# Hybrid attention block on one core: five edits to the order of loads and of VectorE's work (second gate's weights, a third memory weight buffer, the third operand, the end, a half tile)

## The chip, the cores and the metric

The kernel runs on one core of a Trainium2 chip. The metric is device time in microseconds (us). "The time before" is the median of three runs of the kernel before; beside it stands one profiled execution, from which every duration in this document comes.

The core has five engines, each with an instruction stream of its own that is worked off in order: TensorE (PE, matrix multiplies), VectorE (DVE), ScalarE (ACT), GpSimd (POOL) and SyncE (SP), which here only issues transfers. A transfer may also be issued by ScalarE. Engines wait for one another by semaphores.

## The reference, cut to what matters

The input `x` has 1024 rows of width 1024. After an rms norm it is multiplied by one wide weight matrix, and the columns of the product feed three mixers, their gates, and the gates of the merge:

```python
h = rms_norm(x, g_pre[layer])
a_qkv, bq, bk, bv, mq, ga, gb, gm, mg = jnp.split(h @ w_in[layer], split_at, axis=-1)
# A: three groups of heads, dilated windows, merged by a softmax over the groups' log denominators
for gi, (window, dil) in enumerate(A_GROUPS):
    o_g, lse_g = dilated_window_attention(aq[:, :, hs], ak[:, :, hs], av[:, :, hs], window, dil)
wts = jax.nn.softmax(jnp.stack(lses, axis=0), axis=0).astype(dt)
oa = jnp.einsum('gbsh,gbshd->bshd', wts, jnp.stack(outs, axis=0)).reshape(b, s, BRANCH_WIDTH)
# B: grouped queries, rms norms on q and k, axial rope
ob = lax.map(attend, q_blocks).transpose(1, 0, 2, 3, 4, 5).reshape(b, s, B_Q)
# M: cross attention into 256 memory rows
kvm = rms_norm(mem, g_mem[layer]) @ w_mem_kv[layer]
om = jnp.einsum('bhsn,bnhd->bshd', pm, vm).reshape(b, s, M_Q)

ya = (oa * jax.nn.silu(ga)) @ w_br_a[layer]
yb = (ob * jax.nn.silu(gb)) @ w_br_b[layer]
ym = (om * jax.nn.silu(gm)) @ w_br_m[layer]
gates = jax.nn.sigmoid((mg + b_merge[layer]).astype(jnp.float32)).astype(dt).reshape(b, s, N_BRANCHES, d)
merged = gates[:, :, 0] * ya + gates[:, :, 1] * yb + gates[:, :, 2] * ym
x = x + rms_norm(merged @ w_out[layer], g_post[layer])
```

Everything is float32.

## The kernel before, in words

**Arithmetic.** A float32 operand is split into a high part, rounded to the type that TensorE multiplies, and a low part, the rest: ScalarE copies the high part out (`wh`, `hh`), VectorE subtracts it (`wl`, `hl`; both in `split`, L105 to L107). A product is three matmuls: high x high, high x low, low x high. So each weight tile that arrives from memory costs one ScalarE and one VectorE instruction before TensorE can use it. `wr` is the tag of raw weights on arrival, with `WR = 2` buffers; `wh` and `wl` have two each.

**Order.** All of ScalarE's, VectorE's, POOL's and TensorE's work in the parts that the change touches is issued in the order in which the program text issues it (`manual_schedule`). SP's queue is in text order too: a transfer whose buffer isn't free yet holds what stands behind it.

**The start.** `xT` comes in eight tiles `xk[k]` of 128 x 1024 (L448 to L455), tile 0 in two halves; the first half of tile 0 and the whole of tile 1 are issued by ScalarE, all else by SP, between pieces of the weights `wb` of the key and value projection. `x_tile(k)` (L278) splits a tile into `hh[k]`, `hl[k]`, in halves of 512 columns. TensorE runs `kv_proj` (L364): for each `k`, eight row blocks of three 128 x 256 matmuls. Meanwhile the same rows come again in row layout, and ScalarE sums their squares (`row_squares`); POOL makes `rcol` from them (`rstd_cols`), a mean, a power of -0.5, and further small steps. VectorE makes the tables `Ck` and `Sk`, and POOL `Cq` and `Sq`, from one load `bt` (L465).

**The first weave.** L493 runs two gate units on TensorE, two halves of 24 matmuls of 128 x 512 each (`dense`, L140 to L148). Each half ends in a PSUM bank of tag `d`, of which there are two; VectorE empties it into a tile `gth` (L223). A unit's weights are loaded from `wu` and split by `prepare(n)` (L156), which `run_items` calls for unit n and unit n + 1 when unit n begins. Between the matmuls goes other work (`kv_gen`, L407): the key norms `k_norm` (L333: a Square on ScalarE, a sum on VectorE, four small steps `kss` on POOL, products with the tables on VectorE) and the preparation of the memory, `mem_prep` (L383), which reads the transposed memory tiles `mt` (L491) and loads the memory rows into `mr` to sum their squares (L269, L270). After the weave VectorE multiplies the keys by POOL's `kss` (`kn_mult`, L400).

**The memory units.** The second weave (L562) runs eight units `add_kv(u)` of 24 matmuls of 128 x 256 (L537) and one unit of queries. `kv_prep(u)` (L507) loads the unit's weights `wmem[u]` into a `wr` buffer and splits them (L512, L513). In units 1 to 4 a leftover of a gate unit is finished too (`gates_left`): ScalarE's tanh, a product on VectorE, and a store of `gth` to `g2d` (L229), on SP.

**The last item of mixer A.** Mixer A works on 12 items, each in four steps (loop L1751 to L1779): exponentials, scores, masks of the next blocks, transposes `tr` of the probabilities (L1530), copied out as `app` by VectorE (L1534) or ScalarE (L1536), and the values (`pv`, L1539), which fill a `d` bank that ScalarE copies out to `og` (L1560). Behind each step stands filler work, `fill(n)`: n matmuls of the branch products (L1315), which use the same two `d` banks and are emptied by VectorE (L1321). `other(n, j)` (L1661) hangs small work on step j of item n: among it the gated operand k of the branch product, a load (`a_load`), a multiply (`a_mult`, L1597) in place in the tile `ot`, and a split into `hh[k]`, `hl[k]` (`a_split`). Behind the last step (q == NQS) come the turning of the log denominators, `last_weights` (small VectorE steps ending in `leg`), `fill(8)`, and the spreading of the weights by TensorE (`spread`, L1742).

**The end.** The last output block (n = 3, u = 1) is summed and squared in pieces (`piece`, L2060). Its rms norm is a mean of three partial sums (`mean`, L1927 and L1929, on tiles of 128 x 1 in `hbm`), a power on POOL (`root`, L1933), and a product with the residual added (`send_part`, L1962), stored in parts by SP and ScalarE. The gain is multiplied in ahead of that, in three column ranges (`gain`, L1958).

Of the kernel before, what the change touches and what calls it, by code (L numbers as in the profile page):

```python
# [8 lines left out]
F32 = mybir.dt.float32  # L9
# [6 lines left out]
S = 1024  # L16
NT = 8
P = 128
# [32 lines left out]
def block(ctx: ExitStack, tc: tile.TileContext, x, xT, memT, mem, cst, msk, bcst, tabA, gpost,  # L51
          wu, wv, wb, wmem, wbr, wout, out):
    nc = tc.nc
# [4 lines left out]
    wp = ctx.enter_context(tc.tile_pool(name="wp", bufs=2))  # L58
# [20 lines left out]
    def pss1():  # L79
        return bank["p"].tile([P, 512], F32, name="s1", tag="s1", bufs=bank["n"][1])  # L80
# [75 lines left out]
    def prepare(n):  # L156
        if n == len(queue) and n in early and n not in ready:
            ready[n] = early[n]()
        if n < len(queue) and n not in ready:
            ready[n] = queue[n][0]()  # L160
# [84 lines left out]
    def pool(name, side="left"):  # L245
        p = tc.tile_pool(name=name, bufs=1, side=side, reuse_waits="tile")
        return p, p.__enter__()
# [6 lines left out]
    startp, st = pool("start")  # L254
# [10 lines left out]
    xk = [st.tile([P, S], F32, name=f"xk{k}") for k in range(8)]  # L265
# [98 lines left out]
    def kv_proj():  # L364
        banks = [pss1(), pss1(), pss1(), pso()]
        th, tl = wkv
        for k in range(8):
            for T in range(NT):
                dst = banks[T // 2][:, T % 2 * 256:T % 2 * 256 + 256]
                t = slice(T * 128, T * 128 + 128)  # L370
                for i, (a, b) in enumerate([(hh[k][:, t], th[:, k]), (hl[k][:, t], th[:, k]), (hh[k][:, t], tl[:, k])]):
                    PE.matmul(dst, a, b, start=k == 0 and T % 2 == 0 and i == 0, stop=k == 7 and T % 2 == 1 and i == 2)
        return banks
# [74 lines left out]
    for k in range(8):  # L448
        if k in WKV:
            load_wkv(k, WKV[k])  # L450
        if k == 4:
            nc.sync.dma_start(cs, cst)
        for e in range(2 if k == 0 else 1):
            t = slice(e * 512, e * 512 + 512) if k == 0 else slice(0, S)
            (nc.scalar if (k, e) in ((0, 0), (1, 0)) else nc.sync).dma_start(xk[k][:, t], xT[k, :, t])  # L455
    bt = st.tile([P, 1024], F32, name="bt")
    ET = mybir.EngineType
    manual = tc.manual_schedule(engines={ET.Activation, ET.DVE, ET.Pool})
# [26 lines left out]
    table("Ck", B_COS, B_KN, V)  # L485
    table("Sk", B_SIN, B_KS, V)
    banks = kv_proj()
    mt = []
    for c in range(2):
        t = st.tile([P, 4, 256], F32, name=f"mt{c}", tag=f"xk{c}")  # L490
# [14 lines left out]
        V.tensor_copy(mm[1], rows_of(mm[0], 2))  # L505

    def kv_prep(u):  # L507
        raw = wp.tile([P, 1024], F32, name="wr", bufs=WR)
        nc.sync.dma_start(raw, wmem[u])
        wh = wp.tile([P, 1024], R, name="wh")  # L510
        wl = wp.tile([P, 1024], R, name="wl")
        A.activation(wh, raw, AF.Copy)  # L512
        V.tensor_tensor(wl, raw, wh.bitcast(F32), op=OP.subtract)  # L513
        return wh.rearrange("p (k f) -> p k f", k=8), wl.rearrange("p (k f) -> p k f", k=8)
# [291 lines left out]
    lo, hi = half  # L806
# [181 lines left out]
    for n, (i, e, k) in enumerate(steps_v):  # L988
        if k == 0:
            now = v_banks()  # L990
        for j in range(4):
            if i is None:
                t = slice(e * 512 + j * 128, e * 512 + j * 128 + 128)
# [339 lines left out]
    def fill(n):  # L1333
        for _ in range(n):
            next(filler)
        filled[0] += n
# [70 lines left out]
    for f in range(4):  # L1407
        t = t23.tile([P, 2, S], F32, name=f"acc{f}", tag=f"ac{f}")
# [3 lines left out]
    with tc.tile_pool(name="aa", bufs=1, reuse_waits="tile") as aa:  # L1412
# [176 lines left out]
        def a_load(k, both=True):  # L1589
            GG[0, k] = [aa.tile([P, S], F32, name="ot", bufs=2) for _ in range(1 + both)]  # L1590
            for t, src in zip(GG[0, k], (g2d, od)):
                nc.sync.dma_start(t, src[0, k])

        def a_mult(k, o=None, i=slice(0, 64)):
            g_ = GG[0, k][0].rearrange("p (i b) -> p i b", b=16)[:, i]
            o = (GG[0, k][1] if o is None else o).rearrange("p (b i) -> p i b", b=16)[:, i]
            V.scalar_tensor_tensor(g_, o, 0.5, g_, op0=OP.mult, op1=OP.mult)  # L1597

        def a_split(k, t=slice(0, S)):
            assert y_done[0] >= 8  # L1600
            split(hh[k][:, t], hl[k][:, t], GG[0, k][0][:, t])
# [57 lines left out]
        COM = {}  # L1659

        def other(n, j):  # L1661
            p_, g = divmod(n, 3)
            if j == 2:
                if n + 2 < len(items):
                    qk_load(n + 2)
                if n + 1 < len(items):
                    items[n + 1]["values"]()
            if g == 0 and n:
                if j == 0:
                    COM[p_] = combine(p_ - 1)  # L1670
                    COM[p_]["fetch"]()
                elif j == 2:
                    COM[p_]["weights2"]()
                    COM[p_]["load"](0, 1)
            if g == 1 and p_ and j:
                c = COM[p_]
                c["weigh"](j - 1)
                if j == 1:
                    c["load"](2)
                else:  # L1680
                    c["add"](j - 1)
            if g == 2 and j == 0 and 0 < p_ < 3:
                COM[p_]["store"]()
            for k, x in enumerate((0, 1, 2, 4)):
                if (n, j) == (x, 3):
                    b_load(k)
                elif (n, j) == (x + 1, 1):
                    b_split(k)
            for k, q in ((0, 33), (1, 37)):
                x = 4 * n + j - q  # L1690
                if x == 0:
                    a_load(k)
                elif x == 2:
                    a_mult(k)
                elif x == 3:
                    a_split(k)
            if (n, j) == (9, 3):
                a_load(2, False)
            elif (n, j) == (11, 1):
                a_mult(2, COM[3]["ogs"][2])  # L1700
            elif (n, j) == (11, 2):
                a_split(2)
                a_load(3, False)
            if (n, j) == (11, 1):
                lse_load()

# [15 lines left out]
        def last_weights():  # L1722
            mn = cb.tile([P, 2, NT], F32, name="lmn")
            e = cb.tile([P, 3, 2, NT], F32, name="leg")
            dn = cb.tile([P, 3, 2, NT], F32, name="ldn")
            ds_ = cb.tile([P, 2, NT], F32, name="lds")
            V.tensor_tensor(mn, comb[:, 0, :, 0], comb[:, 1, :, 0], op=OP.min)
            V.tensor_tensor(mn, mn, comb[:, 2, :, 0], op=OP.min)
            V.tensor_tensor(e, comb[:, :, :, 0], mn[:, None].to_broadcast([P, 3, 2, NT]), op=OP.subtract)
            A.activation(e, e, AF.Exp, scale=-1.0)  # L1730
            V.tensor_tensor(dn, e, comb[:, :, :, 1], op=OP.mult)
            V.tensor_tensor(ds_, dn[:, 0], dn[:, 1], op=OP.add)
            V.tensor_tensor(ds_, ds_, dn[:, 2], op=OP.add)
            V.reciprocal(ds_, ds_)
            V.tensor_tensor(e, e, ds_[:, None].to_broadcast([P, 3, 2, NT]), op=OP.mult)
            return e
# [14 lines left out]
        for q in range(NQS + 2):  # L1751
            it, j = at(q)
            pr, pj = at(q - 1)
            nx, nj = at(q + 1)
            if it:
                for e in range(2):
                    it["exps"](2 * j + e)
            if nx:
                nx["scores"](nj)
                for e in range(2):  # L1760
                    nx["masked"](2 * nj + e)
            if q == NQS:
                fill(4)
            if pr and q:
                for e in range(2):
                    pr["trans"](2 * pj + e)
            if j == 0 and 0 < q < NQS:
                items[q // 4 - 1]["stats"]()
            if q % 2 and q > 2:
                items[(q - 2) // 4]["pv"]((q - 2) % 4 // 2)  # L1770
            if j == 2 and q // 4 % 3 == 0 and 4 <= q < NQS:
                COM[q // 12]["weights"]()
            if it:
                fill(7 if q % 2 == 0 else 5)
                other(q // 4, j)
            elif q == NQS:
                lse_turn()
                e = last_weights()
                fill(8)  # L1779
        fill(4)  # L1780
        c = combine(3)
# [150 lines left out]
    def root(n, u):  # L1932
        G.tensor_tensor(SS[n, u][:, 3:4], SS[n, u][:, 3:4], mhalf[:, 0:1], op=OP.pow)  # L1933
# [22 lines left out]
    def gain(n, u, c):  # L1956
        r = RES[n, u]
        V.tensor_tensor(r[:, c], r[:, c], gp[:, c], op=OP.mult)  # L1958
# [105 lines left out]
    send_part(3, 0, lo, nc.sync)  # L2064
    piece(0)
    send_part(3, 0, hi, nc.sync)
    gain(3, 1, hi)
    piece(1)
    mean(3, 1, (1, 0))
    gain(3, 1, quarter[0])  # L2070
    mean(3, 1, (2,), False)
    root(3, 1)
    gain(3, 1, quarter[1])
    for c, e in ((hi, nc.sync), (quarter[0], nc.scalar), (quarter[1], nc.sync)):
        send_part(3, 1, c, e)
# [12 lines left out]
WR, KV_STEP, RB_WAIT, KN_PAD = 2, 700, 1500, 2800.0  # L2088
# [119 lines left out]
```

## Time and profile before

| | |
|---|---|
| three runs | 1399.67, 1403.54, 1404.08 us |
| median | 1403.54 us |
| the profiled execution | 1402.44 us, of which its span is 1400.3 us |
| granted TensorE clock, mean | 0.998 |
| transfers | 221.05 MB, 158 GB/s in the mean |

The span runs from the first to the last instruction of the program; the 2.1 us between it and the execution's own time lie around it. Times within the span count from its start. A row of a timeline gives start, duration (both us), engine, line, operation, output <- inputs and shape; the bracket at its end gives how long the engine had stood idle before it and what it had waited for. Small gaps have no bracket, so waits of TensorE are read from the distance between the starts of neighbouring matmuls. A row of the list of waits gives who waited, for whom, and total, count and longest in us. SPq is SP's issuing of a transfer.

### The profile page before, as it was taken

The numbers are of one execution on the slowest core, as the hardware profiler recorded it, in microseconds if no ns is written. First come the engines' busy times: TensorE is split into PE (matmuls) and PEld (weight loads), VectorE is DVE, ScalarE is ACT, GpSimd is POOL, SyncE is SP. The second block draws the span as 40 slices with busy tenths as digits, with TensorE's granted clock in tenths as the row PEclk, the third lists the DMA queues.
The fourth block names the chain that finished last, engine by engine and source line by source line (L and its number), as shares of the span: only waits on it lengthen the run. The fifth ranks groups of instructions, "written<-read, shape, count | busy, mean of one in ns | idle before, by whom it ended". The sixth has DMA issues, their size and how long they took to land.

```text
span 1400.3 us, 21252 instructions
## 1 busy us (share of the span) xinstructions
PE 1383.2 (99%) x7485; PEld 1106.5 (79%) x7485; DVE 977.3 (70%) x1767; ACT 674.6 (48%) x1457; POOL 547.6 (39%) x431
## 2 busy tenths in 40 slices
PE   9999999999999999999999999999999999999997
PEld 8899986666657888888888888888887778778886
DVE  4865458677652387998678777755766656777977
ACT  6644355656653364543222322344446766743453
POOL 1225504676672422267554565423300011245410
PEclk9999999999999999999999999999999999999999
DMA  9432011011005783565555566665567577746613
GB/s 376 141 106 77 16 65 61 17 34 42 17 26 173 265 272 108 177 236 200 140 165 162 166 180 179 204 226 191 200 213 256 175 227 188 256 124 230 228 61 136
DMA packets 108667, 221.05 MB, mean 158 GB/s; under 512 B 20272, under 2 KB 50192, under 8 KB 108560
## 3 DMA queue, kind: packets, MB, share of 16 engines
q1 hardware_dynamic: 94496, 205.14, 45.6%
q10 hardware_dynamic: 14064, 14.55, 3.0%
q8 instruction: 59, 0.97, 0.3%
q14 instruction: 48, 0.39, 0.1%
HBM read 146.97 MB, written 60.09 MB: 148 GB/s over the span
## 4 chain that ended last, share of the span: by engine, by line
PE 85%; DMA 6%; DVE 4%; ACT 2%; issue 2%; SPq 1%; POOL 1%; ACTq 0%; POOLq 0%; DVEq 0%
PE s L1112 35%; PE d L1315 9%; PE s L1901 4%; PE ov L738 4%; PE s L999 3%; PE d L144 3%; PE d L146 3%; PE d L148 3%; PE s L1487 3%; PE d L1550 2%; PE tr L704 2%; PE s L722 2%; PE s L723 2%; PE tr L1530 1%; DMA wr<-in_xT 1%
## 5 line engine op out<-in xcount | busy, mean ns | idle before, releaser
L1112 PE MATMUL s<-T,ch 128*128 128x512 f32 x912 | 215.0, 389 | 0.0
L1112 PEld LDWEIGHTS s<-T,ch 128*128 128x128 f32 x912 | 171.2, 188 | 35.5
L729 POOL TENSOR_TENSOR bl<-bl,bp 128x512 f32<-128x512 f32 x96 | 123.8, 1290 | 48.4 <-ACT bp L725 42.4
L107 DVE TENSOR_TENSOR ch<-sf,ch 128x512 fp32r<-128x512 f32 x102 | 92.6, 914 | 63.2 <-ACT ch L106 63.2
L1112 PE MATMUL s<-hh,ch 128*128 128x512 f32 x408 | 129.8, 389 | 0.0
L1315 PE MATMUL d<-hh,wh 128*128 128x512 f32 x384 | 126.0, 398 | 0.0
L705 DVE TENSOR_REDUCE bn<-tr 128x1 f32<-128x512 f32 x128 | 85.5, 687 | 19.5 <-PE tr L704 18.1
L725 ACT ACTIVATE bp<-s 128x512 f32<-128x512 f32 x128 | 76.0, 597 | 44.9 <-PE s L723 43.2
L1145 POOL TENSOR_TENSOR o<-o,rc 128x1024 f32<-128x1024 f32 x24 | 62.3, 2596 | 70.2 <-DMA o<-rs 53.8
L1112 PEld LDWEIGHTS s<-hh,ch 128*128 128x128 f32 x408 | 76.6, 188 | 15.9
L1177 ACT ACTIVATE sp<-s 128x512 f32<-128x512 f32 x52 | 31.0, 596 | 113.5 <-PE s L1112 93.5
L1315 PEld LDWEIGHTS d<-hh,wh 128*128 128x128 f32 x384 | 72.1, 188 | 15.4 <-issue 0.8
L1322 POOL TENSOR_TENSOR acc<-acc,wl 128x512 f32<-128x512 f32 x32 | 57.1, 1789 | 64.5 <-DVE wl L1321 58.8
L107 DVE TENSOR_TENSOR wl<-wr,wh 128x1024 fp32r<-128x1024 f32 x38 | 51.9, 1365 | 42.6 <-ACT wh L106 40.2
L1112 PE MATMUL s<-hh,wh 128*128 128x512 f32 x208 | 80.9, 389 | 0.0
L1112 PE MATMUL s<-hl,wh 128*128 128x512 f32 x208 | 80.9, 389 | 0.0
L1112 PE MATMUL s<-hh,wl 128*128 128x512 f32 x208 | 80.9, 389 | 0.0
L1112 PE MATMUL s<-hl,ch 128*128 128x512 f32 x204 | 79.4, 389 | 0.0
L106 ACT ACTIVATE wh<-wr 128x1024 fp32r<-128x1024 f32 (+1 forms) x64 | 56.2, 878 | 47.2 <-PE d L1315 15.8
L1505 ACT ACTIVATE pra<-pra,sts 128x192 f32<-128x192 f32 (+2 forms) x176 | 77.4, 442 | 1.6 <-DVE sts L1497 1.6
L1315 PE MATMUL d<-hl,wh 128*128 128x512 f32 x192 | 77.9, 406 | 0.0
L144 PE MATMUL d<-hh,wh 128*128 128x512 f32 x192 | 76.7, 399 | 0.9 <-DVE gth L223 0.9
(415 smaller groups left out, 3599.1 us busy)
## 6 DMA issues: line engine op xcount, KB each, us to landing
wr<-in_wu SPq DMA_DIRECT2D x38, 512.0 KB, 7.2
rw<-in_wu SPq DMA_DIRECT2D x26, 512.0 KB, 5.4
o<-rs SPq DMA_DIRECT2D x96, 128.0 KB, 2.3
qkd<-o SPq DMA_DIRECT2D x24, 512.0 KB, 6.1
wl<-thd SPq DMA_DIRECT2D x24, 512.0 KB, 5.3
thd<-rs ACTq DMA_DIRECT2D x36, 256.0 KB, 2.4
aq<-qkd SPq DMA_DIRECT2D x12, 512.0 KB, 4.6
ak<-qkd SPq DMA_DIRECT2D x12, 512.0 KB, 6.9
```

What stands on the lines that cost most here:

```text
L106: A.activation(dst_h, src, AF.Copy)
L107: V.tensor_tensor(dst_l, src, dst_h.bitcast(F32), op=OP.subtract)
L144: PE.matmul(dst, wh[:, k, :], hh[k][:, t], start=k == 0, stop=False)
L705: fp["last"] = V.tensor_reduce(st[i]["n"][:, j, c:c + 1], s, axis=AX.X, op=OP.min)
L725: A.activation(pp, s, AF.Exp, scale=-1.0)
L729: G.tensor_tensor(lsum[i % 2], lsum[i % 2], pp, op=OP.add)
L738: PE.matmul(o[e * 64:e * 64 + 64], VS[:, kt, kv], d.pop(kt), start=kt < 2, stop=kt >= NT - 2)
L1112: PE.matmul(dst, a, b, start=opens and i == 0, stop=closes and i == 11, skip_group_check=True)
L1145: G.tensor_tensor(QO[n, u], QO[n, u], RT.pop((n, u))[0], op=OP.add)
L1315: PE.matmul(s, a, b, start=q == 0, stop=q == 11)
L1322: G.tensor_tensor(accs[f][:, h], accs[f][:, h], th[:, h], op=OP.add)
L1505: A.activation(src, src, AF.Exp, scale=-1.0, bias=sums(T, h, 0), accum_out=sums(T, h, 1))
```

## The change

It has five edits; line numbers grow by one behind the second.

1. Tile 1 of `xT` is loaded in two halves as tile 0 is: the first by ScalarE, the second by SP.
2. `prepare(1)` stands ahead of the loads of the memory tiles: the second gate unit's weights are loaded and split earlier in the order of SP, ScalarE and VectorE.
3. The third and the sixth memory unit's raw weights go into the buffer `mr`, in which the memory rows were, and no longer into one of the two `wr` buffers.
4. The third operand's multiply is done in two halves, in steps 2 and 3 of the last item and no longer whole in step 1; its split stands behind the last weights and no longer in step 2.
5. At the end, the gain of the last block's second half of columns stands behind the root.

```diff
@@ -450,9 +450,9 @@
             load_wkv(k, WKV[k])
         if k == 4:
             nc.sync.dma_start(cs, cst)
-        for e in range(2 if k == 0 else 1):
-            t = slice(e * 512, e * 512 + 512) if k == 0 else slice(0, S)
-            (nc.scalar if (k, e) in ((0, 0), (1, 0)) else nc.sync).dma_start(xk[k][:, t], xT[k, :, t])
+        for e in range(2 if k < 2 else 1):
+            t = slice(e * 512, e * 512 + 512) if k < 2 else slice(0, S)
+            (nc.scalar if k < 2 and e == 0 else nc.sync).dma_start(xk[k][:, t], xT[k, :, t])
@@ -485,6 +485,7 @@
     table("Sk", B_SIN, B_KS, V)
     banks = kv_proj()
+    prepare(1)
     mt = []
@@ -505,7 +506,7 @@
     def kv_prep(u):
-        raw = wp.tile([P, 1024], F32, name="wr", bufs=WR)
+        raw = st.tile([P, 1024], F32, name="mr", bufs=1) if u % 3 == 2 else wp.tile([P, 1024], F32, name="wr", bufs=WR)
         nc.sync.dma_start(raw, wmem[u])
@@ -1696,11 +1697,10 @@
             if (n, j) == (9, 3):
                 a_load(2, False)
-            elif (n, j) == (11, 1):
-                a_mult(2, COM[3]["ogs"][2])
-            elif (n, j) == (11, 2):
-                a_split(2)
-                a_load(3, False)
+            elif (n, j) in ((11, 2), (11, 3)):
+                a_mult(2, COM[3]["ogs"][2], slice(32 * j - 64, 32 * j - 32))
+                if j == 2:
+                    a_load(3, False)
@@ -1776,6 +1776,7 @@
                 lse_turn()
                 e = last_weights()
+                a_split(2)
                 fill(8)
@@ -2064,12 +2065,12 @@
     piece(0)
     send_part(3, 0, hi, nc.sync)
-    gain(3, 1, hi)
     piece(1)
     mean(3, 1, (1, 0))
     gain(3, 1, quarter[0])
     mean(3, 1, (2,), False)
     root(3, 1)
+    gain(3, 1, hi)
     gain(3, 1, quarter[1])
```

SP's queue from the load of the table `bt` on, of the kernel before (`wu` gate weights, `memT` and `mem` the memory, `wmem` its weights, `g2d` stores of finished gates):

```order
L483 DMA bt<-in_bcst 128x1024
L491 DMA mt_458<-in_memT 128x1024
L491 DMA mt_460<-in_memT 128x1024
L115 DMA wr<-in_wu 128x1024
L269 DMA mr<-in_mem 128x1024
L509 DMA wr<-in_wmem 128x1024 x2
L269 DMA mr<-in_mem 128x1024
L509 DMA wr<-in_wmem 128x1024
L229 DMA g2d<-gth 128x512 x3
L509 DMA wr<-in_wmem 128x1024
L229 DMA g2d<-gth 128x512
```

And with the change:

```order
L483 DMA bt<-in_bcst 128x1024
L115 DMA wr<-in_wu 128x1024
L492 DMA mt_465<-in_memT 128x1024
L492 DMA mt_467<-in_memT 128x1024
L269 DMA mr<-in_mem 128x1024
L510 DMA wr<-in_wmem 128x1024 x2
L269 DMA mr<-in_mem 128x1024
L510 DMA mr<-in_wmem 128x1024
L510 DMA wr<-in_wmem 128x1024
L229 DMA g2d<-gth 128x512 x3
L510 DMA wr<-in_wmem 128x1024
L229 DMA g2d<-gth 128x512
```

The gate weights have moved ahead of the two memory tiles. The third `wmem` load writes to `mr`, behind the second load of memory rows into the same buffer; a fourth `wmem` load now stands ahead of the stores.

TensorE behind the last values of mixer A, with what each row waits for in brackets (`app` transposed probabilities, `avs` values, `hh`/`hl` operands of the branch products, `leg` the last weights), of the kernel before:

```order
L1550 MATMUL d<-app,avs_9520 64x128 [waits DVE_49]
L1550 MATMUL d<-app,avs_9520 64x128
L1315 MATMUL d<-hh_91,wh 128x512 [waits DVE_49]
L1315 MATMUL d<-hl_99,wh 128x512
L1315 MATMUL d<-hh_91,wh 128x512
L1315 MATMUL d<-hh_92,wh 128x512
L1742 MATMUL s_12062<-cs,leg 64x128 x8
```

And with the change:

```order
L1551 MATMUL d<-app,avs_9521 64x128 [waits DVE_49]
L1551 MATMUL d<-app,avs_9521 64x128
L1316 MATMUL d<-hh_91,wh 128x512 [waits Activation_49]
L1316 MATMUL d<-hl_99,wh 128x512
L1316 MATMUL d<-hh_91,wh 128x512
L1316 MATMUL d<-hh_92,wh 128x512
L1742 MATMUL s_12064<-cs,leg 64x128 [waits DVE_49]
L1742 MATMUL s_12064<-cs,leg 64x128 x7
```

The matmuls stand in the same order; the first filler matmul behind the values waits for ScalarE in place of VectorE, and the first spreading matmul has a wait for VectorE of its own.

VectorE at the end, from the first part of the last block but one that is sent (`res` output rows, `on_12606` the gain and `on_12607`/`on_12608` rows of `x`, `wl` the kept sum), of the kernel before:

```order
L1962 SCALAR_TENSOR_TENSOR res<-res,hbm,on_12607 128x512
L1958 TENSOR_TENSOR res<-res,on_12606 128x512
L2061 TENSOR_TENSOR res<-s_13203,wl 128x256
L1927 TENSOR_SCALAR hbm<-hbm 128x1
L1929 SCALAR_TENSOR_TENSOR hbm<-hbm 128x1
L1958 TENSOR_TENSOR res<-res,on_12606 128x256
L1929 SCALAR_TENSOR_TENSOR hbm<-hbm 128x1
L1958 TENSOR_TENSOR res<-res,on_12606 128x256
L1962 SCALAR_TENSOR_TENSOR res<-res,hbm,on_12608 128x512
L1962 SCALAR_TENSOR_TENSOR res<-res,hbm,on_12608 128x256 x2
```

And with the change:

```order
L1963 SCALAR_TENSOR_TENSOR res<-res,hbm,on_12609 128x512
L2062 TENSOR_TENSOR res<-s_13205,wl 128x256
L1928 TENSOR_SCALAR hbm<-hbm 128x1
L1930 SCALAR_TENSOR_TENSOR hbm<-hbm 128x1
L1959 TENSOR_TENSOR res<-res,on_12608 128x256
L1930 SCALAR_TENSOR_TENSOR hbm<-hbm 128x1
L1959 TENSOR_TENSOR res<-res,on_12608 128x512
L1959 TENSOR_TENSOR res<-res,on_12608 128x256
L1963 SCALAR_TENSOR_TENSOR res<-res,hbm,on_12610 128x512
L1963 SCALAR_TENSOR_TENSOR res<-res,hbm,on_12610 128x256 x2
```

The gain of 512 columns has gone from ahead of the last sum to behind the last step of the mean, after which POOL's root starts.

## The prediction

> **What bounds the kernel now.** I read the page's busy times first, then the list of what TensorE waited for, then the places named there. In the first rows the span stands against TensorE's busy time:
>
> ```profile
> span 1400.3 us, 21252 instructions
> PE 1383.2 (99%) x7485; PEld 1106.5 (79%) x7485; DVE 977.3 (70%) x1767; ACT 674.6 (48%) x1457; POOL 547.6 (39%) x431
> ```
>
> TensorE is idle for 17.1 us out of 1400.3, and no edit removes or adds a matmul. So the change can only fill waits of TensorE or shorten the end behind its last matmul. The list of TensorE's waits (total, times, longest, in us) has four rows at places that the change touches:
>
> ```profile
> PE tr L1530 <- DVE app L1534: 1.0, 2, 0.8
> PE d L144 <- DVE gth L223: 0.9, 1, 0.9
> ...
> PE d L537 <- DVE wl L513: 0.8, 1, 0.8
> PE d L537 <- ACT wh L512: 0.7, 1, 0.7
> ```
>
> They add up to 3.4 us. Everything else that I say is about which of them go, and what takes their place.
>
> **Edit 1, the half tile on ScalarE's queue: 0.** The second half of x tile 1 (256 KB) moves from ScalarE's queue to SP's. The stretch view gives 10 to 20 us (columns: length, busy time and instructions of each engine, granted clock, DMA share, GB/s), the timeline two rows of TensorE:
>
> ```profile
> 10.00:20.00 10.00, 10.00 (x90) 10.00 (x90) 9.40 (x15) 8.56 (x15) 0.00 (x0) 1.00 1.04 415
> ```
>
> ```profile
> 6.86 0.39 PE L372 MATMUL s<-wbh,hl 128*128 128x256 f32 x1 [0.41 <-DVE hl L283]
> ...
> 33.62 0.64 PE L275 MATMUL tr<-cs,rcol 128*128 128x128 f32 x4
> ```
>
> The transfer engines are full, so the same bytes take as long in either queue. If the first tile is ready sooner, TensorE starts before 6.86, but it then waits at 33.62 for the row norms, which stand at the end of the same stream (the POOL rows below end them at 33.57). A gain here is therefore lost there. A loss is not: 90 matmuls in 10 us are 0.11 us each, so from 6.86 on the second half of tile 1 is wanted after 36 of them, at 10.8, and from there lateness counts in full. I take 0; bounds -0.2 and +0.6, which is 256 KB at 415 GB/s. [...]
>
> **Edit 2, second gate's weights ahead of the memory tiles: -0.8.** The chain of waits (start, us), then the timelines:
>
> ```profile
> 24.56 10.78 DMA wr<-in_wu
> ...
> 35.36 1.07 ACT wh L106
> ```
>
> ```profile
> 30.76 0.69 DVE L465 TENSOR_TENSOR Ck<-bt,cs 128x512 f32<-128x512 f32 x1 [5.09 <-DMA bt<-in_bcst]
> ```
>
> ```profile
> 31.60 1.97 POOL L131 TENSOR_TENSOR rcol<-rcol,mhalf 128x8 f32<-128x8 f32 x1
> ...
> 35.51 1.10 POOL L465 TENSOR_TENSOR Sq<-bt,cs 128x512 f32<-128x512 f32 x1
> 38.16 0.20 POOL L339 TENSOR_TENSOR kss<-kss,rsq 128x4 f32<-128x4 f32 x1 [1.55 <-DVE kss L338]
> ```
>
> ```profile
> 40.30 0.39 PE L148 MATMUL d<-hh,wl 128*128 128x512 f32 x1
> 41.61 0.50 PE L144 MATMUL d<-hh,wh 128*128 128x512 f32 x1 [0.92 <-DVE gth L223]
> ```
>
> The weights land at 35.34 (24.56 + 10.78), and ScalarE and VectorE stand until then, with the key norms and the first gate's evacuation (gth) queued behind them. TensorE needs that evacuation's bank at 40.53 (40.30 and 0.23 for the matmul) and gets it at 41.61: 1.08 us lost, and 0.1 more in refilling. In the change the weights follow the table bt, which had landed at 30.7; 512 KB at 415 GB/s are 1.26 us, so they land at about 32.0, 3.3 us earlier. VectorE does not gain all of that: its evacuation stands behind a product that waits for POOL's chain from 38.16, and POOL is held by its two tables until 36.6. So at most 38.16 - 36.6 = 1.56 us are free, which would remove the whole stall (-1.2). But VectorE's split, 1.23 us, now runs from 33.1 to 34.3, just as POOL comes from 33.57 to the small steps ahead of the tables. What that does stands elsewhere in the trace:
>
> ```profile
> 120.78 0.27 POOL L318 TENSOR_SCALAR ssb<-ssb,rsq 128x4 f32<-128x4 f32 x1
> ...
> 122.25 1.43 POOL L320 TENSOR_SCALAR ssb<-ssb,rcol 128x4 f32<-128x4 f32 x1
> ```
>
> ```profile
> 121.28 2.35 DVE L107 TENSOR_TENSOR wbl<-wr,wbh 128x1024 fp32r<-128x1024 f32 x2
> ```
>
> Under two such splits a small step of POOL takes 1.43 us in place of 0.27 and ends with the second split (123.63 and 123.68). So POOL loses up to 34.3 - 33.6 = 0.7 us, and its chain starts 0.9 us earlier in place of 1.56. The evacuation then gives the bank free at 41.6 - 0.9 = 40.7, where TensorE wants it at 40.5: -1.0. VectorE's own sums of two SBUF operands, ahead of the evacuation, can be held by the tables in the same way, so I take -0.8; bounds 0 and -1.2. [...]
>
> The memory tiles land one transfer later, some 1.3 us. They are first read by ScalarE behind the key norms, which start earlier too; that covers them.
>
> **Edit 3, a third memory weight buffer: -2.0.** Chain of waits, then TensorE, SP and ScalarE:
>
> ```profile
> 53.88 1.24 DVE wl L513
> 55.14 6.58 DMA wr<-in_wmem
> 61.82 1.07 ACT wh L512
> 62.91 1.24 DVE wl L513
> ```
>
> ```profile
> 61.97 0.28 PE L537 MATMUL d<-mh,wl 128*128 128x256 f32 x1
> 62.93 0.39 PE L537 MATMUL d<-mh,wh 128*128 128x256 f32 x1 [0.69 <-ACT wh L512]
> 63.16 0.28 PE L537 MATMUL d<-ml,wh 128*128 128x256 f32 x1
> 64.19 0.39 PE L537 MATMUL d<-mh,wl 128*128 128x256 f32 x1 [0.76 <-DVE wl L513]
> ```
>
> ```profile
> 50.87 0.33 SPq L509 DMA_DIRECT2D wr<-in_wmem  x1
> ```
>
> ```profile
> 45.48 1.06 ACT L270 ACTIVATE mr<-mr 128x1024 f32<-128x1024 f32 x1 [0.28 <-DMA mr<-in_mem]
> ```
>
> The fourth unit's weights may only be loaded when the second unit's split ends (55.12), take 6.6 us and meet TensorE late. From 61.97 to 64.19, 2.22 us, it issues three matmuls of 0.11: 1.9 us lost, and 0.1 in refilling. In the change the third unit's weights go into the buffer of the memory rows, free from 46.5 (45.48 + 1.06), and the fourth takes the place that the third has in SP's queue now, at 50.87, 4.3 us before 55.14. It then lands by 57.5, and the wait goes. What is late next is the fifth unit, now issued at 55.14 or before: even with 6.6 us it lands by 61.7 and its two splits (1.07, 1.24) end by 64.1. It is wanted 24 x 0.11 = 2.7 us after the fourth starts at 62.1, less the 0.8 of edit 2: at 64.0. So it just fits with the same delay. I take -2.0; bounds -2.0 and 0. SP issues in order, and its wait for ScalarE's square at 46.5 now stands ahead of the fourth unit's load; that load is not due before 50.87, which covers it.
>
> **Edit 4, the third operand in halves and its split later: -0.3.**
>
> ```profile
> 1239.80 2.01 DVE L1597 SCALAR_TENSOR_TENSOR ot<-og,ot 128x1024 f32<-128x1024 f32 x1
> ```
>
> ```profile
> 1241.84 0.38 PE L1530 MATMUL tr<-cs,pra 128*128 128x128 f32 x2
> 1243.04 0.44 PE L1530 MATMUL tr<-cs,pra 128*128 128x128 f32 x2 [0.82 <-DVE app L1534]
> ...
> 1249.55 1.09 PE L1550 MATMUL d<-app,avs 128*64 128x128 f32 x16
> 1250.60 0.50 PE L1315 MATMUL d<-hh,wh 128*128 128x512 f32 x1
> ```
>
> ```profile
> 1250.69 0.60 ACT L1560 ACTIVATE og<-d 128x512 f32<-128x512 f32 x1 [1.94 <-PE d L1550]
> ```
>
> The multiply of 2.01 us stands ahead of the masks and the copy that TensorE waits for at 1243.04. Two transposes take 0.2, the start-to-start is 1.20: 1.0 us lost. In halves, behind those copies, it no longer stands there: -1.0. But the order of the change shows a new wait: TensorE's first filler matmul behind the last values (1250.60) now waits for ScalarE and no longer for VectorE. The only ScalarE step left there is the copy og of the bank just written. It starts 0.05 after the last values end (1250.64) and takes 0.60, so TensorE, ready at 1250.60, could go at 1251.3: +0.7. Sum -0.3; bounds -1.0 (the copy is not what it waits for) and +0.2 (it waits for the evacuation behind the moved split: 1.06 and 1.22 us on ScalarE and VectorE).
>
> **Edit 5, the end's order: -0.3.**
>
> ```profile
> 1393.23 0.68 DVE L1958 TENSOR_TENSOR res<-res,on 128x512 f32<-128x512 f32 x1
> ...
> 1395.82 1.54 DVE L1962 SCALAR_TENSOR_TENSOR res<-res,hbm,on 128x512 f32<-128x512 f32 x3 [0.44 <-POOL hbm L1933]
> ```
>
> ```profile
> 1389.55 0.93 POOL L1933 TENSOR_TENSOR hbm<-hbm,mhalf 128x1 f32<-128x1 f32 x1 [8.75 <-DVE hbm L1929]
> 1395.12 0.67 POOL L1933 TENSOR_TENSOR hbm<-hbm,mhalf 128x1 f32<-128x1 f32 x1 [4.63 <-DVE hbm L1929]
> ```
>
> The gain of 0.68 (0.60 between starts) leaves the place ahead of the last sum and comes behind the mean, so the root starts 0.6 earlier. There it runs beside a wide gain and not a narrow one: 0.93 in place of 0.67. Left: -0.34; bounds -0.6 and 0.
>
> **The sum.** 0 - 0.8 - 2.0 - 0.3 - 0.3 = -3.4 us, since TensorE is full from the places of edits 2 and 3 to the end, and later waits hang on it, not on the clock. The profiled execution took 1402.44 us (span 1400.3), which gives 1399.0. The median shown, 1403.54, would give 1400.1; its runs lie from 1399.67 to 1404.08. I take the middle, 1399.6.
>
> **Rivals.**
> - *The middle gains in full* (0.18): the matmul at 1250.60 does not wait, edit 4 is -1.0 and edit 2 -1.2. For it: VectorE's own release was in time. Against: the wait in the order. 1402.44 - 4.5 = 1397.9, or 1398.5 by the same middle.
> - *The gate stall stays* (0.20): POOL holds the evacuation, edit 2 is 0. For it: even with the gain as reckoned the bank is 0.2 us late. Against: 3.3 us of earlier landing. -2.6: 1400.4.
> - *The third buffer does nothing* (0.07): the fourth unit's weights are still slow, edit 3 is 0. For it: 6.58 us for one load. Against: 4 us of earlier issue. -1.4: 1401.6.
> - *Slower* (0.05): the half tile behind SP's queue misses the first projection. TensorE has no slack from 6.86 to 33.62, so each us after 10.8 costs one. It decides from 3.4 us late, at 14.2; 5 us late, 1404.0, or 1404.6 by the same middle. For it: SP's queue is in order and full. Against: only three small pieces stand ahead of it.
>
> **How the numbers follow.** My forecast has 0.50. A change within 0.3% (4.2 us) is what a measurement here can hardly tell from none. The forecast lies inside that, 0.8 us from its edge, with runs that scatter by 2 us: a third of it falls beyond. Faster by over 0.3%: 0.50 x 0.35 + 0.18 x 0.7 + 0.20 x 0.2 + 0.07 x 0.1 = 0.35. Slower by over 0.3%: 0.03. Within: 0.62. The range is 1396.3 to 1402.9: below, the full middle and the low runs; above, the third buffer's failure.
>
> **What would show it.** Right: the second gate's split on ScalarE near 32, not 35.4; no wait of TensorE at the fourth memory unit; the wait at the transposes of the last item gone and one of some 0.7 us at the filler matmul behind the last values, ended by og; the last root some 0.6 us nearer to the last matmul. Wrong: the wait for gth still near 1 us, or later waits of TensorE that grow by what the first 70 us gained.

## The result, and the profile after

| | kernel before | changed kernel |
|---|---|---|
| median (lowest to highest) of 22 runs each | 1401.17 us (1398.14 to 1405.00) | 1398.53 us (1397.06 to 1402.11) |
| ratio, 95% interval | | 0.9983, 0.9976 to 0.9991 |
| profiled execution, its span | 1402.44, 1400.3 | 1401.02, 1399.2 |

The change makes the kernel faster by 0.17%, some 2.4 us (1.3 to 3.4). The stated range, 1396.3 to 1402.9, holds the time; the sum of the terms was -3.4. By the bound of 0.3% this is no difference, the likeliest of the three outcomes.

The list of TensorE's waits after the change, below its first two rows (who, for whom, total, times, longest in us):

```profile
PE s L1000 <- ACT wh L106: 0.9, 1, 0.9
PE d L1316 <- ACT wh L106: 0.8, 1, 0.8
PE d L1316 <- ACT og L1561: 0.7, 1, 0.7
PE s L1000 <- DVE wh L107: 0.6, 1, 0.6
PE s L1113 <- DVE rs L1158: 0.6, 1, 0.6
```

The four rows on which the prediction rested (tr for app, d for gth, and two for the memory weights wl and wh) are gone. The wait for og, which the order foretold, has come. Three others are new and stand at places that no edit touches: the first row (near 487 us), the second (near 1050) and the last (near 916).

Rows picked from the timeline of the changed kernel, at the gate and at the fourth memory unit:

```profile
32.53 1.06 ACT L106 ACTIVATE wh<-wr 128x1024 fp32r<-128x1024 f32 x1 [1.32 <-DMA wr<-in_wu]
34.17 0.73 POOL L377 TENSOR_TENSOR rsq<-rcol 128x8 f32<-128x8 f32 x1
35.94 0.96 DVE L347 TENSOR_TENSOR kt<-kt,kt 128x256 f32<-128x256 f32 x1
40.45 0.69 DVE L223 TENSOR_TENSOR gth<-d,rb 128x512 f32<-128x512 f32 x1
41.95 0.39 PE L148 MATMUL d<-hh,wl 128*128 128x512 f32 x1
42.18 0.39 PE L144 MATMUL d<-hh,wh 128*128 128x512 f32 x1
50.44 0.33 SPq L510 DMA_DIRECT2D wr<-in_wmem  x1
59.37 1.06 ACT L513 ACTIVATE wh<-wr 128x1024 fp32r<-128x1024 f32 x1 [0.27 <-PE d L538]
62.34 0.28 PE L538 MATMUL d<-mh,wh 128*128 128x256 f32 x1
62.57 0.28 PE L538 MATMUL d<-mh,wl 128*128 128x256 f32 x1
```

The second gate's split runs at 32.53 (35.36 before). The 42.18 row is the matmul that waited until 41.61 before; it follows its forerunner by 0.23, without a wait. The fourth memory unit's split waits for TensorE (for the buffer of split weights) and no longer for a transfer.

At the last item and at the end:

```profile
1241.50 0.60 PE L1531 MATMUL tr<-cs,pra 128*128 128x128 f32 x4
...
1249.30 0.60 ACT L1561 ACTIVATE og<-d 128x512 f32<-128x512 f32 x1 [0.33 <-PE d L1551]
1249.95 0.50 PE L1316 MATMUL d<-hh,wh 128*128 128x512 f32 x1 [0.70 <-ACT og L1561]
...
1393.85 0.93 POOL L1934 TENSOR_TENSOR hbm<-hbm,mhalf 128x1 f32<-128x1 f32 x1 [4.03 <-DVE hbm L1930]
1394.81 1.54 DVE L1963 SCALAR_TENSOR_TENSOR res<-res,hbm,on 128x512 f32<-128x512 f32 x3
```

Two transposes and the two behind them run through (the second pair stood at 1243.04 before); the filler matmul behind the last values waits 0.70 for og, and starts at 1249.95. The last root starts 1.35 behind TensorE's last end (1392.50) in place of 1.95. (Between the two places of edit 4, L1707 to L1777, the change does not shift the line numbers.)

### The profile page after: what moved, and what is told of

It reads as the page before. It is cut to its first block, busy times and chain, and to the rows that moved or that the text cites. A ratio compares the mean times of both kernels' runs of the same rounds, so it can differ in the third digit from the quotient of the medians.

```text
span 1399.2 us, 21259 instructions
## 1 busy us (share of the span) xinstructions
PE 1383.4 (99%) x7485; PEld 1108.6 (79%) x7485; DVE 983.8 (70%) x1768; ACT 673.5 (48%) x1457; POOL 545.1 (39%) x431
## 4 chain that ended last, share of the span: by engine, by line
PE 86%; DMA 5%; DVE 4%; ACT 2%; issue 2%; SPq 1%; POOL 0%; ACTq 0%; POOLq 0%; DVEq 0%
PE s L1113 30%; PE d L1316 10%; PE s L1902 4%; PE ov L739 4%; PE s L1000 3%; PE d L144 3%; PE d L148 3%; PE d L146 3%; PE s L1488 3%; PE d L1551 3%; PE tr L705 2%; PE s L723 2%; PE s L724 2%; PE d L538 2%; PE tr L1531 2%
## 5 line engine op out<-in xcount | busy, mean ns | idle before, releaser
L730 POOL TENSOR_TENSOR bl<-bl,bp 128x512 f32<-128x512 f32 x96 | 123.6, 1287 | 48.6 <-ACT bp L726 42.5
L107 DVE TENSOR_TENSOR ch<-sf,ch 128x512 fp32r<-128x512 f32 x102 | 97.3, 960 | 61.6 <-ACT ch L106 61.6
L1316 PE MATMUL d<-hh,wh 128*128 128x512 f32 x384 | 126.0, 398 | 1.5 <-ACT wh L106 0.8
L148 PE MATMUL d<-hh,wl 128*128 128x512 f32 x192 | 76.7, 400 | 0.0
```

The lines of the kernel that those rows point to most:

```text
L107: V.tensor_tensor(dst_l, src, dst_h.bitcast(F32), op=OP.subtract)
L148: PE.matmul(dst, wl[:, k, :], hh[k][:, t], start=False, stop=k == 7)
L730: G.tensor_tensor(lsum[i % 2], lsum[i % 2], pp, op=OP.add)
L1316: PE.matmul(s, a, b, start=q == 0, stop=q == 11)
```

## The experiments

Each kernel below has a profile of its own; where a ratio is given, it was also timed in turn with the kernel before (10 to 12 runs of it against 14 to 23). The others were run once, so what is said of them rests on one profile. To compare the profiles I take three times of TensorE in each: the start of the projection's last matmul (L372, the 192nd), the start of one matmul behind the first query unit's weights (call it Q; 80.37 in the kernel before), and the end of the last matmul. "Half rate" is the stretch after 7 us in which the projection's matmuls start 0.21 apart and not 0.11.

| kernel (edits) | half rate until | projection's last | Q | from there to Q | last matmul ends |
|---|---|---|---|---|---|
| before (none) | not at all | 28.51 | 80.37 | 51.86 | 1393.17 |
| before, again (none) | 9.5 | 29.92 | 80.44 | 50.52 | 1394.16 |
| half_tile_only (1) | 10.6 | 30.43 | 80.91 | 50.48 | 1392.78 |
| operand_and_end (4, 5) | 11.1 | 30.32 | 80.98 | 50.66 | 1393.28 |
| gate_only (2) | 12.7 | 32.25 | 81.39 | 49.14 | 1393.85 |
| third_buffer_only (3) | not at all | 30.03 | 78.32 | 48.29 | 1390.58 |
| front_two (2, 3) | 10.9 | 31.11 | 79.36 | 48.25 | 1390.46 |
| without_half_tile (2 to 5) | 9.6 | 29.82 | 78.42 | 48.60 | 1389.43 |
| changed (all) | 11.2 | 30.22 | 78.73 | 48.51 | 1392.50 |
| changed, again (all) | 10.6 | 31.27 | 79.51 | 48.24 | 1391.41 |
| split_behind_fill (all, split later) | not at all | 29.16 | 77.64 | 48.48 | 1392.19 |
| warm_before (none, more warming) | 7.5 | 29.76 | 79.83 | 50.07 | 1393.28 |
| warm_changed (all, more warming) | not at all | 29.19 | 77.47 | 48.28 | 1390.78 |
| warm_and_split (all, both) | not at all | 28.42 | 77.75 | 49.33 | 1388.88 |

**Both kernels once more.** No edit. Two theories of the half rate in the changed kernel's first profile stand against each other: A, it is chance from run to run; B, the half tile causes it.

> The kernel before, once more, to see which waits of TensorE repeat. [...] Of the waits that the changed kernel has and the kernel before has not (0.9 at the split of a weight near 487 us, 0.6 near 916, 0.8 near 1050): if they are chance, one or more of them shows here too, and the waits at 40.5 (1.1) and 62 to 64 (1.9) stand unchanged.

> The changed kernel, once more. Theory A: the half clock at the start (1.7 us) is absent or elsewhere; Theory B: it is there again, from about 8 us for 3.3 us. The wait behind the last values that ScalarE's copy og ends (0.7) is fixed by the order and must be there again. The waits near 487, 916 and 1050 us: if the shift of the front by 3 us makes them, all three come again; if they are chance, they come in part.

Busy time of TensorE in the projection's matmuls by stretches (length; TensorE and its weight loads, busy time and count; granted clock; DMA share; GB/s), of the kernel before in its first profile, in its second, and of the changed kernel in its first:

```profile
7.00:8.00 1.00, 1.00 (x10) 1.00 (x10) 1.00 1.06 368
8.00:9.00 1.00, 1.00 (x11) 1.00 (x10) 1.00 0.98 401
```

```profile
7.00:8.00 1.00, 1.00 (x5) 1.00 (x6) 1.00 0.96 324
8.00:9.00 1.00, 1.00 (x7) 1.00 (x6) 1.00 1.03 405
9.00:10.00 1.00, 1.00 (x7) 1.00 (x7) 1.00 1.03 401
```

```profile
7.00:8.00 1.00, 1.00 (x9) 1.00 (x10) 0.98 0.99 334
8.00:9.00 1.00, 1.00 (x7) 1.00 (x6) 0.50 1.04 416
10.00:11.00 1.00, 1.00 (x7) 1.00 (x7) 0.50 1.07 392
```

Ten or eleven matmuls against seven in a stretch of a microsecond, where one that only reaches into the stretch counts too; by their starts, 0.113 and 0.213 apart, it is about nine against five. The unedited kernel runs at half rate too, and its first profile was one of the few that did not. The changed kernel does it in both profiles, without edit 1 as well. So theory A stands, with a stronger turn: half rate is the usual start (8 of the 11 profiles with the old warming), not the exception. The second profile of the kernel before shows what that does to the gate. The evacuation in the first profile, then the timeline of the second, and its waits:

```profile
40.88 0.68 DVE L223 TENSOR_TENSOR gth<-d,rb 128x512 f32<-128x512 f32 x1
```

```profile
40.81 0.68 DVE L223 TENSOR_TENSOR gth<-d,rb 128x512 f32<-128x512 f32 x1
...
41.65 0.39 PE L148 MATMUL d<-hh,wl 128*128 128x512 f32 x1
41.88 0.39 PE L144 MATMUL d<-hh,wh 128*128 128x512 f32 x1
```

```profile
PE tr L1530 <- ACT app L1536: 1.6, 1, 1.6
...
PE d L144 <- ACT wh L106: 0.6, 1, 0.6
...
PE d L148 <- DVE wl L107: 0.5, 1, 0.5
...
PE d L537 <- DVE wl L513: 0.4, 1, 0.4
```

The evacuation gth runs when it ran before, but TensorE comes 1.4 later and does not wait for it. Against the first profile TensorE is 1.4 late at the projection's end, wins 1.1 at the gate, 0.3 in a refill and 1.3 at the memory unit (0.4 of waiting in place of 1.5), and loses 1.4 to the query unit's weights (the rows L144 and L148). So Q is at 80.4 in both. The expectation that the waits at 40.5 and 62 to 64 stand unchanged was wrong. Of the three late waits that the changed kernel had, those near 916 (0.2) and 1050 (1.0) came again in its second profile and the one near 487 did not; the kernel before has that one in its second profile.

**Edits 2 and 3, apart and together.**

```diff
     banks = kv_proj()
+    prepare(1)
```

```diff
-        raw = wp.tile([P, 1024], F32, name="wr", bufs=WR)
+        raw = st.tile([P, 1024], F32, name="mr", bufs=1) if u % 3 == 2 else wp.tile([P, 1024], F32, name="wr", bufs=WR)
```

> Edit 2 alone. The wait for gth near 41 us goes (-1.1 and 0.3 of refilling after a start without half clock; with half clock at the start the kernel before has no such wait either, and then edit 2 gains nothing there). The fourth memory unit still waits: if edits 2 and 3 are independent 1.9 us at 62 to 64; if edit 2 only moves TensorE earlier into a wait that the weights set, more than that, by what edit 2 gained, and the net at 65 us is 0.

> Edit 3 alone. The wait for gth stays if the clock at the start is full (1.1), and is absent if it is at half for 3 us; the wait at the fourth memory unit is gone either way (-0.5 to -1.9). The wait at the transposes near 1146 us (1.2), which the kernel before has twice and all kernels with edits 2 and 3 lack: gone here if it hangs on edit 3's time, there if it hangs on edit 2's.

> Edits 2 and 3 alone. By my terms -2.8 (0.8 and 2.0), by what the changed kernel's trace shows -3.3 (1.43 and 1.88) up to 65 us. If both are independent of the other edits, the waits for gth and for the fourth memory unit are gone here too and the multiply's wait at 1243 (1.0) is still there. Ratio 0.9977 to 0.998 if the gain holds to the end; nearer to 1 if later waits take it back.

The gate in the kernel with the third buffer alone, which has no edit there (timeline), and the only wait for memory weights that is left with edit 2 alone:

```profile
41.80 0.39 PE L148 MATMUL d<-hh,wl 128*128 128x512 f32 x1
42.03 0.39 PE L144 MATMUL d<-hh,wh 128*128 128x512 f32 x1
```

```profile
PE d L538 <- DVE wl L514: 0.2, 1, 0.2
```

With edit 3 alone no wait for gth is left, since the projection ended at 30.03 (at full rate, but after a wait of 0.7 near 8.2 us for the split of the first tile's second half); from the projection's end to Q it takes 48.3 us, as long as with both edits. With edit 2 alone Q is at 81.39: its start was the latest of all, and it says only that edit 2 does not bring Q below 80. The two edits together, timed, gave 0.9992 (0.9980 to 1.0003), 1.1 us where I expected 2.8 to 3.3. The interval does not exclude a gain of 2.8, just.

In the table the kernels without edit 3 reach Q between 79.8 and 81.0, whether the projection ends at 28.5 or at 30.4 (81.4 where it ends at 32.3): weights set it. With edit 3 the distance is 48.2 to 48.6 in seven of eight: TensorE sets it. (The eighth, 49.3, has the earliest projection of all and waits 0.4 at 34.1 us for the row norms.) Edit 3 so takes Q from the weights' time to TensorE's, and what it is worth depends on the start: with the old warming Q is at 80.8 in the mean of the five profiles without edit 3 and at 78.7 in that of the six with it, 2.1 us, while the projection ends at 30.3 in the mean of both groups. Since the kernel with edit 3 alone has the same distance as those with both, no run here shows that edit 2 adds to this. The gain reaches the end: the last matmul ends at 1392.8 to 1394.2 us in all six profiles without edit 3 and at 1388.9 to 1392.5 in all eight with it.

The wait near 1146 us, after which the expectations ask, is absent with edit 2 alone, with edit 3 alone and with edit 1 alone, so it shows nothing of edits 2 and 3.

**Edit 1.**

```diff
-        for e in range(2 if k < 2 else 1):
-            t = slice(e * 512, e * 512 + 512) if k < 2 else slice(0, S)
-            (nc.scalar if k < 2 and e == 0 else nc.sync).dma_start(xk[k][:, t], xT[k, :, t])
+        for e in range(2 if k == 0 else 1):
+            t = slice(e * 512, e * 512 + 512) if k == 0 else slice(0, S)
+            (nc.scalar if (k, e) in ((0, 0), (1, 0)) else nc.sync).dma_start(xk[k][:, t], xT[k, :, t])
```

> The change without edit 1 (tile 1 whole on ScalarE's queue, as before). Theory A: the same time as the changed kernel within 0.1%, ratio to the kernel before 0.998; no steady difference in the first 12 us other than the clock's. Theory B: 1.2 to 1.7 us faster than the changed kernel, ratio 0.997, and no half clock at the start.

> Edit 1 alone. If it is worth nothing: TensorE's first real matmul between 5.85 and 6.4 us as in the eight traces so far, no wait of TensorE for the halves of tile 1 between 7 and 13 us, and from 80 us on TensorE stands where the kernel before has it (80.4, 80.5). If the half tile comes late: a wait near 10.8 us of up to 0.6.

Without the half tile the ratio is 0.9988 (0.9977 to 0.9998), within 0.1% of the changed kernel's, and half rate comes all the same: theory B falls. With the half tile alone Q is at 80.91, and the waits on the way are of the kinds that the kernel before has in its second profile, among them

```profile
PE d L537 <- DVE wl L513: 0.8, 1, 0.8
...
PE d L148 <- DVE wl L107: 0.5, 1, 0.5
```

No wait of TensorE for a half of tile 1 was seen. Edit 1 is worth nothing that these runs can tell. One thing may speak against it: the rows' stream, by the start of VectorE's table Ck behind it, ends at 31.1 us in the mean of the six profiles with edit 1 and at 30.7 in that of the eight without. The two groups overlap (30.8 to 31.4 and 30.3 to 31.2), and no run separates the edit from chance there.

**Edits 4 and 5.** The two alone, as in the diff of the change.

> Edits 4 and 5 alone. The wait at the transposes near 1243 us goes (-1.0 to -1.1), a wait of 0.7 for the copy og comes behind the last values, net -0.4; from TensorE's last matmul to the last output part issued 0.4 less than the kernel before has (4.55 from 1393.17 to the end of the last issue at 1397.72). The front as in the kernel before: a wait at the fourth memory unit of 0.5 to 1.9.

```profile
PE d L1315 <- ACT og L1560: 0.7, 1, 0.7
```

TensorE gains 1.01 at the transposes and loses 0.67 at the filler matmul: -0.34, and in the changed kernel -1.04 and +0.67. From TensorE's last end to the end of the last issue it takes 4.22 here and in every kernel with edit 5 (4.21 or 4.22), and 4.55 in every kernel without: -0.33. Both terms came as worked out; nothing of them can be seen in the time of one run.

Then the split one place later:

```diff
                 e = last_weights()
-                a_split(2)
                 fill(8)
+                a_split(2)
```

> The changed kernel with the third operand's split one place later, behind the eight filler steps. In the order VectorE's emptying of the filler bank then stands ahead of that split again, and the next filler matmul waits for VectorE as in the kernel before. If the 0.7 comes from the bank that the order picks: no wait of TensorE behind the last values, 0.67 less than the changed kernel from there to the end. If VectorE's split itself is the price: the wait only changes its releaser to VectorE (1.0 or more).

From the list of its waits, and its timeline around the last values:

```profile
PE d L1316 <- DVE wl L1322: 0.6, 1, 0.6
```

```profile
1245.07 1.98 POOL L1323 TENSOR_TENSOR acc<-acc,wl 128x512 f32<-128x512 f32 x1 [4.36 <-DVE wl L1322]
...
1246.27 0.82 DVE L1727 TENSOR_TENSOR lmn<-comb 128x16 f32<-128x16 f32 x1
...
1248.80 0.21 DVE L1735 TENSOR_TENSOR leg<-leg,lds 128x48 f32<-128x48 f32 x1
1248.92 0.68 DVE L1322 SCALAR_TENSOR_TENSOR wl<-wl,d 128x512 f32<-128x512 f32 x1
...
1249.66 0.50 PE L1316 MATMUL d<-hh,wh 128*128 128x512 f32 x1 [0.61 <-DVE wl L1322]
```

The same places in the kernel before:

```profile
1247.85 0.18 DVE L1727 TENSOR_TENSOR lmn<-comb 128x16 f32<-128x16 f32 x1 [0.18 <-ACT comb L1719]
...
1249.86 0.68 DVE L1321 SCALAR_TENSOR_TENSOR wl<-wl,d 128x512 f32<-128x512 f32 x1
```

Neither expectation was right. The split no longer stands ahead of the evacuation, but the evacuation starts only when the chain of the last weights ends on VectorE, at 1249.0. Before, the evacuation ended at 1250.54 and TensorE was ready for the bank at 1250.60. Here TensorE is ready 1.5 earlier, at 1249.05, but the evacuation comes only 0.9 earlier and ends at 1249.60, so TensorE waits 0.59 in place of 0.67. The price of edit 4 is not the bank that the order picked; it is VectorE's chain, which is next behind the wait that was removed.

The chain loses 0.64 at its first step, which takes 0.82 in place of 0.18, about as much as the evacuation has fallen behind TensorE. It ends at 1247.09, just as POOL's sum ends (1247.05), and that sum takes 1.98 in place of the 1.27 that it takes in the kernel before. VectorE's multiply of the operand's second half (1.04 from 1244.91) runs beside the sum's start. This is the same kind of holding up between POOL and VectorE as at the gate (0.73 for 0.20 and 0.96 for 0.46 there), and it is there in the changed kernel too (0.82 and 1.98). So edit 4 seems to have slowed the chain that TensorE then waits for; no run took that apart.

**More warming.** To see whether half rate ends earlier with eleven warming matmuls in place of eight, and whether the time follows. In its two profiles the projection of the kernel before ends 1.4 apart (28.51 and 29.92); counted in full, that is a ratio of 0.9990.

```diff
-WARM = 8
+WARM = 11
```

> The kernel before with 11 warming matmuls in place of 8, so that TensorE is busy up to its first real matmul at 6.0. [...] If the front of the kernel before is bound by TensorE after all: ratio 0.9990.

> The changed kernel with 11 warming matmuls. [...] If the clock at the start is chance that more warming does not move: as the changed kernel.

> The changed kernel with 11 warming matmuls and the split behind the filler steps. If both gains add: 0.7 less than with the warming alone, ratio to the kernel before 0.997 (0.9971 from 0.9976), and no wait of TensorE of more than 0.3 us behind the last values. If later waits take one of them back: 0.9976 again.

The projection's matmuls by stretches, of the kernel before and of the changed kernel, both with 11 warming matmuls:

```profile
7.00:8.00 1.00, 1.00 (x6) 1.00 (x7) 1.00 0.99 369
8.00:9.00 1.00, 1.00 (x11) 1.00 (x10) 1.00 1.01 414
```

```profile
7.00:8.00 1.00, 1.00 (x11) 1.00 (x10) 1.00 0.95 336
8.00:9.00 1.00, 1.00 (x11) 1.00 (x10) 1.00 1.04 426
```

Half rate is over by 7.7 in all three (the clock's first record of full speed stands at 7.74, 4.35 and 5.35 us). The kernel before gains nothing by it: 1.0007 (0.9998 to 1.0016), with a wait of 0.8 for the fourth memory unit as ever. The changed kernel has Q at 77.47, 1.3 and 2.0 earlier than in its own two profiles, and 0.9976 (0.9967 to 0.9986). With the later split as well Q is at 77.75 and the ratio 0.9979 (0.9969 to 0.9988): the second gain does not show, as the 0.59 above says. That more warming brings the changed kernel to Q earlier is what the traces say; that it makes the whole kernel faster isn't shown, since the intervals (0.9976 to 0.9991 against 0.9967 to 0.9986) do not separate the two.

## Why the prediction held, and where its terms did not

- **Edit 1, 0:** held, as far as these runs can tell.
- **Edit 2, -0.8:** the mechanism held. The split came at 32.53, POOL's small step stretched behind VectorE's split (0.73 for 0.20), a VectorE sum behind POOL's table (0.96 for 0.46), and gth came 0.43 earlier while the rows' stream ended 0.5 later, so 0.9 against that, as reckoned. The other profiles say the same: from the start of the table Ck to the start of gth it is 10.1 in all six without edit 2, and 9.2 in seven of the eight with it (8.9 in the eighth). The size did not hold: the step "TensorE needs that evacuation's bank at 40.53" was read from a profile with a fast start. With the usual start TensorE is there at 41.9, and there is no wait to remove.
- **Edit 3, -2.0:** the wait went in full, in each kernel with the edit. But after a usual start the kernel before waits 0.4 to 0.8 there, and loses the rest to the query unit's weights. That this later wait is removed too, since all weights behind the third come earlier, was not in the working.
- **Edits 2 and 3 together, -2.8:** mis-sized. After a fast start it is right: Q at 77.5 to 77.8 in the three kernels with the edits and a projection that ends by 29.2, against 80.37, which is 2.6 to 2.9. But the shares differ: behind the gate TensorE stands only 0.5 ahead there (41.14 to 41.18 against 41.61), and the memory unit brings 2.0. After the starts that came it was 2.1 in the traces, by the comparison with and without edit 3. The sentence "TensorE is full from the places of edits 2 and 3 to the end" left out that TensorE is not always on time at these places.
- **Edit 4, -0.3:** -0.34 to -0.37, with both parts as worked out (-1.0, +0.7). **Edit 5, -0.3:** -0.33, with the root at 0.93 as taken.
- **The sum, -3.4:** by the traces -2.1 - 0.4 - 0.3 = -2.8; measured -2.4 (1.3 to 3.4 faster). The predicted 1399.6 stands 1.1 above the measured median, and that it is so near is in part luck: the middle from which it was reckoned amounts to 1403.0 for the kernel before, whose median over 22 runs is 1401.17, so 1.8 too high, while the gain was taken too large by 0.8 to 1.0. The two errors work against each other.

Of the rivals, "the gate stall stays" named the right gain for that edit (0) by the wrong mechanism: nothing holds the evacuation, TensorE is late for it.

**What is left open.** From Q to the last matmul the 14 profiles take 1311.0 to 1314.6 us. The difference lies in waits that come and go: at the transposes near 1146 us 1.2 in the first profile of the kernel before, 2.0 in its second and none in both of the changed kernel; near 1050 us up to 1.2, near 641 us 1.3 in one profile alone. Those near 487, 916 and 1146 us stand behind a split or a product that had waited for a transfer (`wr` from `xT`, 8.0, and `ak` from `g2d`, 4.8, in the changed kernel; `ot` from `od`, 2.5, in the kernel before), but no edit decides them one way in all profiles, and I have not found what does. They are as large as the gain, so a single pair of profiles (spans 1400.3 and 1399.2) does not measure this change.

## What to carry to other kernels

A stall in one profile is worth what the profile's own start makes of it. Before a wait is priced, take a second profile of the unchanged kernel and see whether the engine that waits comes on time (here the 0.9 for gth in the first profile was not in the second), and look for the place where two profiles with different starts meet again (here Q, at 80.37 and 80.44): up to there something else sets the time. An engine that is freed by a microsecond can wait for the next chain on its way (here TensorE was ready 1.5 earlier and waited 0.59): look at the end of that chain, not only at the instruction that is moved.

## What the runs showed of the hardware

**TensorE's clock at the start.** In the changed kernel's first profile the warming matmuls and the first real ones stand so:

```profile
2.53 2.48 PE L447 MATMUL d<-wl 128*128 128x512 f32 x6
6.17 0.38 PE L372 MATMUL s<-wbh,hh 128*128 128x256 f32 x1 [1.16 <-ACT hh L282]
6.96 0.38 PE L372 MATMUL s<-wbh,hl 128*128 128x256 f32 x1 [0.40 <-DVE hl L283]
7.18 0.28 PE L372 MATMUL s<-wbl,hh 128*128 128x256 f32 x1
```

The first row is the last six of the eight warming matmuls, and ends at 5.01. The rate is full at 7.2 (matmuls 0.11 apart), half from 8.0 to 11.2 (0.21 apart, 0.50 in the rows of stretches above) and full again. The clock's own records in this profile are full from 4.55, half from 7.96 and full from 11.38, 3.41 apart; between the first two TensorE had worked for 0.5 + 0.4 + 1.0 us. In operand_and_end they are full from 4.58, half from 7.99 and full from 11.40. third_buffer_only, with its first record of full speed at 5.74, kept the full rate. In the other six profiles with half rate the first record of full speed stands at 9.87 to 12.99.

The same kernel starts differently from run to run: the kernel before has no half rate in its first profile and half rate until 9.5 in its second, the changed kernel has it until 11.2 and until 10.6. What raises the clock and what lowers it was not shown; of what may act on it only more warming was tried (half rate over by 7.7 in three profiles).

The column of the granted clock does not always show this: the kernel before, in its second profile, has 1.00 beside matmuls that start 0.213 apart. The first record of the clock in that trace stands at 9.87, and the column gives 1.00 ahead of it.

**A second rate.** After the start the projection's matmuls were 0.118 apart in seven of the 14 profiles and 0.113 in the other seven, with no edit common to either. Over the projection's 192 matmuls that is about 0.9 us. What decides it was not tried.
